# Low parts of the exponentials on GpSimd, and the values' low part as a full weight tile

## The chip, the cores and the metric

The kernel runs on one core of one Trainium2 chip. The metric is the device time of one execution in microseconds: 2285.27 us, the median of three runs (2280.55 to 2286.03). The profile of before is of a separate execution.

## The reference, cut to what matters

The model is a two-layer diffusion backbone over 1024 latent tokens and 256 context tokens, width 1024. Layer 0 runs grouped-query attention (8 query heads of 64, 2 key/value heads) beside a bidirectional mLSTM (4 heads of 128), then a mixture of 16 experts; layer 1 is a pooling mixer and a second mixture of experts. The change touches attention alone:

```python
qb = q.reshape(Bn, nb, Q_BLOCK, A_KV_HEADS, G, d).transpose(1, 0, 3, 4, 2, 5)   # G = 4 heads per key head
def one_block(qblk):
    s = jnp.einsum('bhgtd,bhsd->bhgts', qblk, kt).astype(jnp.float32) * scale
    p = jax.nn.softmax(s, axis=-1).astype(vt.dtype)
    return jnp.einsum('bhgts,bhsd->bhgtd', p, vt)
```

The keys and values are those of the 256 context tokens followed by the 1024 latent tokens, so each of the 8 heads weighs 1280 keys for 1024 queries. Everything is float32.

## The kernel before, in words

A float32 product is made of three faster matmuls. `split` (L57) writes a rounded high part (type fp32r) on ScalarE and the rest, source minus high part, on VectorE (L59, L60). A product is then high x high + high x low + low x high, each a matmul of fp32r operands. A plain float32 matmul is also used in places; it shows as two instructions.

The kernel runs in stages: projections of layer 0 (to about 390 us), `mixers` (attention and mLSTM, to about 732 us), `out0` (the output projection, norm and router), the experts of layer 0, `layer1`, and the experts of layer 1.

`attention_start` (L593) runs interleaved with the last projection. For each of the two key heads g it makes KS (keys, high part in partitions 0 to 63 and low part in 64 to 127), K2 (high part, and a row of ones for the bias), VA (128 keys x 10 tiles x 128: the values' high part in columns 0 to 63, ones in columns 64 to 127) and VL (128 x 10 x 64: the values' low part). They lie in the pool `kv`, allocated from the right end of SBUF.

`mixers` (L676) walks over the 8 heads. For head h, `weighted(h)` takes two query blocks of 512 and for each of them ten key tiles of 128. A tile is two matmuls for the scores (L703, L704) into one of two PSUM buffers `se`, the exponential on ScalarE (L706, `e`), and the weighted values into `po`, where rows 0 to 63 collect the output and rows 64 to 127 the sum of the weights. Three of the ten tiles (`WHOLE`: 2, 5, 8) use one plain float32 matmul of `e` with VF (L709). For the other seven, `e` is split into `eh` and `el`: by `split` (ScalarE and VectorE) in heads 0 to 6, and on VectorE alone (L717, L718) in head 7. Then come three matmuls: VA x eh (L719), VL x eh into rows 0 to 63 only (L720), and VA x el (L721). `e`, `eh` and `el` have three buffers each. Two block ends per head take a reciprocal of the sum through Ln and Exp (L724, L725), one product on VectorE (`oo`, L727) and a store.

Beside head h run the preparation of head h+1 (`queries`, L626; `largest`, L645: the scores once more, with a maximum per query on VectorE from PSUM, L659 and L664, and the maxima sent through a small DMA to the bias row of QB, L674, issued on GpSimd) and the steps of the mLSTM (`mlstm`, L764). On GpSimd there stand in this stage only the memsets of QB (L635), v (L774) and VF (L693) and that DMA.

The order of each engine's instructions is made before the run by the framework's scheduler: it takes the program's order as priority, issues what it finds ready by its own costs, and adds every wait. Each engine then executes its list in order. A tile's memory can be reused once the earlier tile there is released.

Of the kernel before, what the change touches and what calls it, by code (L numbers as in the profile page):

```python
# [11 lines left out]
F32 = mybir.dt.float32  # L12
F32R = mybir.dt.float32r
# [4 lines left out]
ALU = mybir.AluOpType  # L18
# [8 lines left out]
NTA = 10  # L27
# [16 lines left out]
class Kern:  # L44
# [548 lines left out]
    def attention_start(self, es, psp):  # L593

        tc, nc = self.tc, self.nc
        P = lambda name, bufs=1: es.enter_context(tc.tile_pool(name=name, bufs=bufs, side="right", reuse_waits="tile"))
        P("pad").tile([128, PADS[2]], F32, name="pad")
        kv, self.q0, self.qs = P("kv"), P("q0"), P("qs", 2)
        self.q1 = None
        self.at = self.sc = (psp, "tr")  # L600
        KS = self.KS = [kv.tile([128, 1280], F32R, name=f"KS{g}") for g in range(2)]
        K2 = self.K2 = [kv.tile([128, 1280], F32R, name=f"K2{g}") for g in range(2)]
        VA = self.VA = [kv.tile([128, NTA, 128], F32R, name=f"VA{g}") for g in range(2)]
        VL = self.VL = [kv.tile([128, NTA, 64], F32R, name=f"VL{g}") for g in range(2)]
        self.Q = {}
        for g in range(2):
            nc.gpsimd.memset(K2[g][64:128].bitcast(F32), 0.0)
            nc.gpsimd.memset(K2[g][64:65].bitcast(F32), 1.0)
            nc.gpsimd.memset(VA[g][:, :, 64:128].bitcast(F32), 1.0)
        for g in range(2):  # L610
            if g:
                self.queries(0)
                yield
                yield from self.largest(0)
            for c0, c1 in ((0, 4), (4, 8), (8, 10)):
                ps = self.at[0].tile([128, 512], F32, name=self.at[1], tag=self.at[1])
                for t in range(c0, c1):
                    nc.tensor.transpose(ps[0:64, (t - c0) * 128:(t - c0 + 1) * 128],
                                        self.KR[:, t, g * 64:(g + 1) * 64], self.idf)
                s = slice(c0 * 128, c1 * 128)  # L620
                self.halves(ps[0:64, :(c1 - c0) * 128], KS[g][0:64, s], K2[g][0:64, s], KS[g][64:128, s])
                yield
            self.split(VA[g][:, :, 0:64], VL[g], self.VR[:, :, g * 64:(g + 1) * 64])
            yield

    def queries(self, h):  # L626
# [48 lines left out]

    def mixers(self):  # L676
        tc, nc, I = self.tc, self.nc, self.I
        KS, K2, VA, VL, Q = self.KS, self.K2, self.VA, self.VL, self.Q
        with ExitStack() as es:
            P = lambda name, bufs=1, **k: es.enter_context(tc.tile_pool(name=name, bufs=bufs, reuse_waits="tile", **k))  # L680
            ml = P("ml", 2)
            pp, sp, self.q1 = P("p", 3), P("ast", 2), P("q1")
            ps_t, ps_s = P("ps_t", 1, space=PSUM), P("ps_s", 2, space=PSUM)
            ps_e, ps_o, ps_m = P("ps_e", 2, space=PSUM), P("ps_o", 1, space=PSUM), P("ps_m", 2, space=PSUM)
            self.at, self.sc = (ps_t, "at"), (ps_s, "sc")

            def weighted(h):

                QA, QB = Q.pop(h)
                g = h // 4  # L690
                if h % 4 == 0:
                    self.VF = sp.tile([128, len(WHOLE), 128], F32, name="VF", tag="VF", bufs=1)
                    nc.gpsimd.memset(self.VF[:, :, 64:128], 1.0)  # L693
                    for i, t in enumerate(WHOLE):
                        nc.vector.tensor_copy(self.VF[:, i, 0:64], self.VR[:, t, g * 64:(g + 1) * 64])
                VF = self.VF
                for q in range(2):
                    qs = slice(q * 512, (q + 1) * 512)
                    po = ps_o.tile([128, 512], F32, name="po", tag="po")
                    for t in range(NTA):  # L700
                        ts = slice(t * 128, (t + 1) * 128)
                        ps = ps_e.tile([128, 512], F32, name="se", tag="se")
                        nc.tensor.matmul(ps, KS[g][:, ts], QA[:, qs], start=True, stop=False)  # L703
                        nc.tensor.matmul(ps, K2[g][:, ts], QB[:, qs], start=False, stop=True)  # L704
                        e = pp.tile([128, 512], F32, name="e", tag="e")
                        nc.scalar.activation(e, ps, AF.Exp)  # L706
                        a, l = t == 0, t == NTA - 1
                        if t in WHOLE:
                            nc.tensor.matmul(po, VF[:, WHOLE.index(t)], e, start=a, stop=l, skip_group_check=True)  # L709
                            yield  # L710
                            continue
                        eh = pp.tile([128, 512], F32R, name="eh", tag="eh")
                        el = pp.tile([128, 512], F32R, name="el", tag="el")
                        if h < 7:
                            self.split(eh, el, e)
                        else:
                            nc.vector.tensor_copy(eh, e)  # L717
                            nc.vector.tensor_tensor(el, e, eh.bitcast(F32), op=ALU.subtract)  # L718
                        nc.tensor.matmul(po, VA[g][:, t], eh, start=a, stop=False, skip_group_check=True)  # L719
                        nc.tensor.matmul(po[0:64], VL[g][:, t], eh, start=False, stop=False, skip_group_check=True)  # L720
                        nc.tensor.matmul(po, VA[g][:, t], el, start=False, stop=l, skip_group_check=True)  # L721
                        yield
                    rc = sp.tile([64, 512], F32, name="rc", tag="rc")
                    nc.scalar.activation(rc, po[64:128], AF.Ln)  # L724
                    nc.scalar.activation(rc, rc, AF.Exp, scale=-1.0)  # L725
                    o = sp.tile([64, 512], F32, name="oo", tag="oo")
                    nc.vector.tensor_tensor(o, po[0:64], rc, op=ALU.mult)  # L727
                    nc.sync.dma_start(self.OT[h * 64:(h + 1) * 64, qs], o)

            M = self.mlstm_steps(ml, ps_m)  # L730
            for h in range(8):
                nxt = iter(())
                if h < 7:
                    self.queries(h + 1)
                    nxt = self.largest(h + 1)
                for i, _ in enumerate(weighted(h)):
                    for _ in range(2 if i % 5 == 0 else 1):
                        next(nxt, None)
                    if i % 5 == 4:
                        next(M, None)  # L740
            for _ in M:
                pass
# [910 lines left out]
```

## Time and profile before

| | |
|---|---|
| median of the runs | 2285.27 us (2280.55 to 2286.03) |
| the profiled execution | 2288.23 us |
| its span, first to last instruction | 2286.4 us |
| mean granted TensorE clock | 0.966 of 2.4 GHz |
| busy over the span | PE 93%, DVE 82%, ACT 62%, POOL 10% |

PE is TensorE, PEld its weight loads, DVE VectorE, ACT ScalarE, POOL GpSimd. A matmul's duration in the records includes its way through the array, so durations of successive matmuls overlap; how fast they follow each other is read from their starts. In the rows below, a wait is named by who waited, for what, and what released it; brackets in the timeline give the idle time of the engine before the instruction and what ended it.

### The profile page before, as it was taken

How to read it: one execution, taken by the hardware profiler on the slowest of the kernel's cores; microseconds unless marked ns; L12 is line 12 of the kernel's file. 1: busy time of each engine (PE TensorE's matmuls, PEld its weight loads, DVE VectorE, ACT ScalarE, POOL GpSimd, SP SyncE). 2: the span in 40 equal slices, each digit the busy share in tenths (PEclk: the TensorE clock that was granted, in tenths of full speed). 3: DMA queues.
4: the chain of work that ended last, by engine and by line, in shares of the span. 5: the costliest groups of instructions: out<-in, count | busy, mean ns of one | idle time of the engine just before them, and what ended most of it. 6: DMA issues, size and time to landing. Idle time of an engine off the chain costs nothing.

```text
span 2286.4 us, 29558 instructions
## 1 busy us (share of the span) xinstructions
PE 2120.9 (93%) x10371; PEld 1678.5 (73%) x10371; DVE 1884.3 (82%) x2936; ACT 1408.8 (62%) x2042; POOL 220.8 (10%) x345
## 2 busy tenths in 40 slices
PE   6889999999997988999999999899659999999997
PEld 3768887776664767788888877667548888888874
DVE  7888754888886557899999989844589999999986
ACT  6412314667774325788888877744337888888874
POOL 0111111000000011000000000012200000000001
PEclk9999999999998999999999999989869999999998
DMA  7576662243413658999999999513869999999964
GB/s 276 187 253 229 243 217 92 79 120 95 111 58 95 246 193 318 392 393 393 402 393 392 401 375 356 184 33 102 314 225 359 393 399 391 397 391 390 397 227 157
DMA packets 211738, 609.76 MB, mean 267 GB/s; under 512 B 17620, under 2 KB 62116, under 8 KB 210436
## 3 DMA queue, kind: packets, MB, share of 16 engines
q1 hardware_dynamic: 168800, 484.95, 56.0%
q0 software_dynamic: 22560, 79.61, 11.8%
q10 hardware_dynamic: 20228, 43.30, 5.2%
q8 instruction: 82, 1.34, 0.2%
q14 instruction: 68, 0.56, 0.1%
HBM read 550.11 MB, written 56.77 MB: 265 GB/s over the span
## 4 chain that ended last, share of the span: by engine, by line
PE 77%; DMA 8%; DVE 6%; issue 5%; ACT 3%; POOL 1%; ACTq 0%; POOLq 0%; DVEq 0%; SPq 0%
PE g L54 5%; PE g L55 5%; PE u L54 5%; PE g L53 5%; PE u L53 5%; PE d L54 5%; PE u L55 5%; PE d L55 5%; PE d L53 5%; DMA wm<-in_w_mod 2%; PE tr L1250 2%; PE pp L55 2%; PE pp L54 2%; PE pp L53 2%; PE po L709 2%
## 5 line engine op out<-in xcount | busy, mean ns | idle before, releaser
L60 DVE TENSOR_TENSOR wl<-R,wh 128x1024 fp32r<-128x1024 f32 x496 | 584.7, 1222 | 26.0 <-ACT wh L59 13.7
L59 ACT CAST wh<-R 128x1024 fp32r<-128x1024 f32 x496 | 518.1, 1055 | 131.1 <-PE g L55 43.0
L60 DVE TENSOR_TENSOR wl<-X,wh 128x1024 fp32r<-128x1024 f32 x182 | 215.9, 1222 | 13.8 <-ACT wh L59 8.7
L59 ACT CAST wh<-X 128x1024 fp32r<-128x1024 f32 x182 | 190.4, 1054 | 49.3 <-PE d L55 22.6
L53 PE MATMUL u<-wh,xh 128*128 128x512 f32 x512 | 202.7, 396 | 2.5 <-ACT wh L59 2.5
L53 PE MATMUL d<-wh,ah 128*128 128x512 f32 x512 | 201.8, 394 | 2.9 <-DVE o L1285 2.9
L53 PE MATMUL g<-wh,xh 128*128 128x512 f32 x512 | 202.6, 396 | 1.7 <-ACT xh L59 1.7
L54 PE MATMUL u<-wl,xh 128*128 128x512 f32 x512 | 201.2, 393 | 2.3 <-DVE wl L60 2.2
L54 PE MATMUL d<-wl,ah 128*128 128x512 f32 x512 | 200.5, 392 | 2.3 <-DVE wl L60 2.3
L54 PE MATMUL g<-wl,xh 128*128 128x512 f32 x512 | 200.8, 392 | 2.0 <-DVE wl L60 1.9
L55 PE MATMUL u<-wh,xl 128*128 128x512 f32 x512 | 200.6, 392 | 0.0
L55 PE MATMUL g<-wh,xl 128*128 128x512 f32 x512 | 200.3, 391 | 0.0
L55 PE MATMUL d<-wh,al 128*128 128x512 f32 x512 | 199.9, 390 | 0.0
L59 ACT CAST wh<-raw 128x1024 fp32r<-128x1024 f32 (+1 forms) x116 | 119.7, 1039 | 54.6 <-PE pp L55 12.4
L60 DVE TENSOR_TENSOR wl<-raw,wh 128x1024 fp32r<-128x1024 f32 (+1 forms) x116 | 135.9, 1204 | 11.6 <-ACT wh L59 8.8
L706 ACT ACTIVATE e<-se 128x512 f32<-128x512 f32 x160 | 91.5, 595 | 56.8 <-PE se L704 50.6
L54 PEld LDWEIGHTS u<-wl,xh 128*128 128x128 f32 x512 | 96.6, 189 | 24.0 <-DVE wl L60 4.8
L54 PEld LDWEIGHTS d<-wl,ah 128*128 128x128 f32 x512 | 96.3, 188 | 23.4 <-DVE wl L60 4.6
L53 PEld LDWEIGHTS d<-wh,ah 128*128 128x128 f32 x512 | 96.3, 188 | 22.8 <-ACT ah L59 3.7
L54 PEld LDWEIGHTS g<-wl,xh 128*128 128x128 f32 x512 | 96.5, 189 | 22.3 <-DVE wl L60 3.4
L53 PEld LDWEIGHTS u<-wh,xh 128*128 128x128 f32 x512 | 96.6, 189 | 22.2 <-ACT wh L59 2.9
L53 PEld LDWEIGHTS g<-wh,xh 128*128 128x128 f32 x512 | 96.5, 189 | 21.6 <-ACT xh L59 2.7
(523 smaller groups left out, 4710.8 us busy)
## 6 DMA issues: line engine op xcount, KB each, us to landing
R<-in_w_exp_gate SPq DMA_DIRECT2D x84, 1024.0 KB
R<-in_w_exp_down SPq DMA_DIRECT2D x82, 1024.0 KB
R<-in_w_exp_up SPq DMA_DIRECT2D x81, 1024.0 KB
wm<-in_w_mod POOLq DMA_DIRECT2D x80, 512.0 KB, 5.4
X<-in_w_exp_up SPq DMA_DIRECT2D x31, 1024.0 KB
X<-in_w_exp_gate SPq DMA_DIRECT2D x30, 1024.0 KB
X<-in_w_exp_down SPq DMA_DIRECT2D x30, 1024.0 KB
raw<-in_w_exp_up SPq DMA_DIRECT2D x16, 1024.0 KB
```

The source lines that it names most:

```text
L53: mm(ps, lh, rh, start=start, stop=False)
L54: mm(ps, lh, rl, start=False, stop=False)
L55: self.mark = mm(ps, ll, rh, start=False, stop=stop).ins
L59: self.nc.scalar.copy(hi, src)
L60: return self.nc.vector.tensor_tensor(lo, src, hi.bitcast(F32), op=ALU.subtract).ins
L706: nc.scalar.activation(e, ps, AF.Exp)
L709: nc.tensor.matmul(po, VF[:, WHOLE.index(t)], e, start=a, stop=l, skip_group_check=True)
L1250: nc.tensor.transpose(ps[:, j * 128:(j + 1) * 128], src[:, (4 * q + j) * 128:(4 * q + j + 1) * 128], self.idf)
```

## The change

In heads 0 to 6 the high part `eh` stays on ScalarE, and the subtraction that makes `el` is issued on GpSimd. Head 7 stays as it was. VL becomes a tile of 128 columns like VA; columns 64 to 127 are zero, and its matmul writes all 128 rows of `po`. VL moves from the pool `kv` (right side, allocated before the projections end) to the pool `ast` of `mixers` (left side), from 2 x 2560 to 2 x 5120 bytes a partition. Two memsets on GpSimd write the zeros; the subtraction that makes VL, formerly part of `split` in `attention_start`, is done on VectorE at the first head of each group. The copy of the high part into VA stays on ScalarE where it was.

```diff
@@ attention_start
-        VL = self.VL = [kv.tile([128, NTA, 64], F32R, name=f"VL{g}") for g in range(2)]
...
-            self.split(VA[g][:, :, 0:64], VL[g], self.VR[:, :, g * 64:(g + 1) * 64])
+            nc.scalar.copy(VA[g][:, :, 0:64], self.VR[:, :, g * 64:(g + 1) * 64])
@@ mixers
+            VL = [sp.tile([128, NTA, 128], F32R, name=f"VL{g}", bufs=1) for g in range(2)]
+            for g in range(2):
+                nc.gpsimd.memset(VL[g][:, :, 64:128].bitcast(F32), 0.0)
@@ weighted, where h % 4 == 0
+                    nc.vector.tensor_tensor(VL[g][:, :, 0:64], self.VR[:, :, g * 64:(g + 1) * 64],
+                                            VA[g][:, :, 0:64].bitcast(F32), op=ALU.subtract)
@@ weighted, per tile
                         if h < 7:
-                            self.split(eh, el, e)
+                            nc.scalar.copy(eh, e)
+                            nc.gpsimd.tensor_tensor(el, e, eh.bitcast(F32), op=ALU.subtract)
...
-                        nc.tensor.matmul(po[0:64], VL[g][:, t], eh, start=False, stop=False, skip_group_check=True)
+                        nc.tensor.matmul(po, VL[g][:, t], eh, start=False, stop=False, skip_group_check=True)
```

## Rows read from the trace of the kernel before

**Rows 1.** Windows, 400 to 700: length, busy us (count) by engine, clock, DMA.

```profile
400.00:700.00 300.00, 284.11 (x1400) 205.31 (x1399) 265.38 (x594) 214.06 (x498) 11.52 (x33) 0.99 0.34 92
```

**Rows 2.** Waits, 400 to 700: us in total, times, longest.

```profile
POOL v L774 <- PE mp L833: 174.2, 16, 17.0
...
POOL QB L674 <- DMA md<-mr: 46.4, 2, 38.1
...
PEld se L703 <- ACT e L706: 14.2, 29, 1.5
...
PEld po L721 <- DVE el L60: 4.1, 9, 1.5
...
PE po L721 <- DVE el L60: 1.5, 2, 1.0
PE se L704 <- DMA QB<-md: 1.5, 1, 1.5
...
PEld po L719 <- ACT e L706: 0.7, 3, 0.2
...
PE sc L663 <- DVE mx L659: 0.4, 1, 0.4
```

**Rows 3.** Groups by line and form, 400 to 700: busy us, mean ns, idle before.

```profile
L60 DVE TENSOR_TENSOR el<-e,eh 128x512 fp32r<-128x512 f32 x96 | 65.3, 685 | 4.4 <-ACT eh L59 4.1
...
L719 PEld LDWEIGHTS po<-eh,VA 128*128 128x128 f32 x96 | 18.1, 189 | 13.7 <-ACT eh L59 6.2 <-issue 2.2 <-DVE oo L727 2.1
...
L720 PEld LDWEIGHTS po<-eh,VL 128*64 128x64 f32 x96 | 13.1, 136 | 5.6 <-issue 4.3
...
L828 DVE TENSOR_TENSOR v<-v,g_col 128x516 f32<-128x516 f32 x17 | 11.8, 693 | 0.7 <-PE mp L814 0.5
...
L817 DVE TENSOR_TENSOR dn<-dn,g_col 128x2 f32<-128x2 f32 x32 | 4.9, 154 | 5.8 <-ACT dn L816 5.5
```

**Rows 4.** Groups by line and form, POOL, whole span.

```profile
L951 POOL TENSOR_TENSOR h<-h,r_a 128x1024 f32<-128x1024 f32 x2 | 4.7, 2334 | 0.1
...
L609 POOL MEMSET VA<- 128x640 f32 x2 | 1.3, 640 | 20.6 <-PE tr L574 17.4 <-DVE KS L748 3.1
...
L1047 POOL TENSOR_TENSOR res<-aff,tk 128x128 f32<-128x128 f32 x2 | 0.9, 459 | 0.0
```

**Rows 5.** Timeline, two split tiles near 505: start us, us, instruction.

```profile
503.84 0.61 ACT L59 CAST eh<-e 128x512 fp32r<-128x512 f32 x1
...
504.71 0.69 DVE L60 TENSOR_TENSOR el<-e,eh 128x512 fp32r<-128x512 f32 x1
...
505.45 0.19 PEld L721 LDWEIGHTS po<-el,VA 128*128 128x128 f32 x1
...
506.43 0.62 ACT L59 CAST eh<-e 128x512 fp32r<-128x512 f32 x1
...
507.99 0.69 DVE L60 TENSOR_TENSOR el<-e,eh 128x512 fp32r<-128x512 f32 x1
...
508.86 0.19 PEld L721 LDWEIGHTS po<-el,VA 128*128 128x128 f32 x1
```

**Rows 6.** Timeline, GpSimd and VectorE side by side near 856.

```profile
855.39 2.33 POOL L951 TENSOR_TENSOR h<-h,r_a 128x1024 f32<-128x1024 f32 x1
...
856.08 1.66 DVE L1019 TENSOR_TENSOR thr<-nxt,tm 128x4 int32<-128x4 int32 x1
857.67 0.15 DVE L997 TENSOR_TENSOR base<-base,tm 128x1 int32<-128x1 int32 x1
```

**Rows 7.** Timeline, PE, matmuls of one tile in a row, near 722.

```profile
722.11 0.39 PE L719 MATMUL po<-eh,VA 128*128 128x512 f32 x1
722.34 0.39 PE L720 MATMUL po<-eh,VL 128*64 128x512 f32 x1
722.56 0.39 PE L721 MATMUL po<-el,VA 128*128 128x512 f32 x1
```

**Rows 8.** Timeline, VectorE after the end of attention.

```profile
736.99 0.29 DVE L892 TENSOR_TENSOR wp<-wr,a2c 128x128 f32<-128x128 f32 x1 [4.72 <-DMA wr<-in_w_router]
```

More of the change, by code (lines that the diff above doesn't have):

```diff
@@ L677, in mixers @@
         tc, nc, I = self.tc, self.nc, self.I
-        KS, K2, VA, VL, Q = self.KS, self.K2, self.VA, self.VL, self.Q
+        KS, K2, VA, Q = self.KS, self.K2, self.VA, self.Q
         with ExitStack() as es:
```

## The prediction

> **What bounds the kernel now.** I read the page's busy shares first, then the stages by windows, then the waits, the groups and the timeline of the stage that the diff touches. The reader is to see in the busy shares only that no engine is the limit of the whole span; the change lies in one stage. From 400 to 700 us the heads before the last run beside the mLSTM steps. There DVE works 265.4 of 300 us (88%), ACT 214.1, PE is marked busy for 284.1, and GpSimd for 11.5 [rows 1]. So this stage has a nearly full DVE and an empty GpSimd, and the change takes work from the first to the second.
>
> A full engine need not be the one that the path waits for, so the waits decide. PE executes its instructions in a fixed order, and a wait of PE or of its weight load is lost time unless the matmul before it is still streaming. In this stage eight such groups of waits are ended by ACT, from 14.2 for the score buffers that the exponential still reads down to 0.7: 37.5 us. Eleven groups are ended by DVE: from 4.1 for `el` down to 0.4 for a maximum, together 16.0, of which `el` itself is 4.1 + 1.5 = 5.6 in 11 cases [rows 2]. PE thus waits for ACT more than twice as much as for DVE, although DVE is the fuller one. That is what keeps my forecast small: at most 16.0 us can go directly, and 53.5 if ACT's waits went too.
>
> **The change part by part.**
>
> *The subtraction leaves DVE.* In heads 0 to 6 fourteen query blocks have seven split tiles each, 98 in all; 96 of them start in the window, at 685 ns: 65.3 us [rows 3]. DVE falls to 200.1 us of 300.
>
> *It arrives on GpSimd.* The trace has no subtraction of 128x512 there. It has the two-source form at 128x128 (459 ns) and at 128x1024 (2334 ns) [rows 4]; these are the bounds. A straight line between them gives 459 + 384/896 x 1875 = 1263 ns, which I take, since both ends are the same kind of operation and the new one lies between; that the output is now fp32r is not in any row. 98 x 1.263 = 124 us, on an engine with 288 us free here: throughput is no limit. Latency is: each low part takes 1.263 - 0.685 = 0.58 us longer.
>
> *Who feels these 0.58 us.* Two tiles show both answers [rows 5]. The first `eh` ends at 504.45, DVE begins 0.26 later, and PE loads `el` at 505.45, at once when it is there; GpSimd would finish at about 505.76, 0.3 us late. The second `eh` ends at 507.05, DVE is in other work until 507.99 and delivers at 508.68; GpSimd would deliver at about 508.4, earlier than DVE, and PE asks for it only at 508.86. Bounds: none of the low parts is late, or all 96 are by the whole difference, 56 us. Only 11 of 96 wait today, so I am near the lower end: these 11 cost 6.4 us more; a fresh queue without DVE's backlog gives about a third of it back, +4 us.
>
> *A lock beside it.* While GpSimd's multiplication at 855.39 reads its two SBUF sources, DVE's 128x4 tensor operation takes 1.66 us and ends as GpSimd ends; a like one behind it takes 0.15 [rows 6]. So a DVE operation with two SBUF sources stands still until GpSimd is through. In the window eight groups have two such sources (v, E twice, wi, the output projection's low parts, hs, ob, dn): 141 instructions, 73.5 us; the first and the last are in [rows 3]. GpSimd will be in a subtraction 96 x 1.263 / 300 = 40% of the time, with 0.63 us left on average: 141 x 0.40 x 0.63 = 36 us more on DVE. Bounds 0 and 96 x 1.263 = 121 us, if every subtraction held DVE throughout. I take the 36: DVE 236 of 300, 79% instead of 88%. So more than half of what DVE seems to gain is taken back.
>
> The Trainium skill, "SBUF — State Buffer", section "Who interferes with whom", says that it goes the other way too: whichever comes first holds the pair, so a subtraction can also stand behind DVE. No row shows GpSimd held; by that rule each would meet such an operation with chance 73.5/300, about 0.1 us on average or 9 us of latency over all, most of it in tiles that PE doesn't yet ask for.
>
> *GpSimd's queue.* It runs in order, too, and today its waits cost nothing because nothing stands behind them: 174.2 us in 16 waits of the v memset for PE, and 46.4 in 2 of the query bias load for a small DMA [rows 2]. Now subtractions stand behind them, and behind each subtraction that waits for `eh` the next QB and v memsets and the bias load, for which the next head's scores wait. The order is made ahead of the run from when things become ready, so a subtraction should not stand long behind a later event: 0 at best, 23 such instructions (16 and 7) with 1.26 us each at worst, 29; I take 0, since PE waits for the bias load once, 1.5 us.
>
> *The freed DVE.* DVE's other results (maxima, wi, oo) come earlier. Of 10.4 us that PE waits for them I let two thirds go, -7: the load of DVE that is left is 79%. ACT, too, waits for DVE (E, sq, the e buffers held by `el`), and the exponentials behind these are what PE waits for longest; of the 37.5 us I let a fifth go, -7. Bounds: 0 and -10.4 for the first, 0 and -37.5 for the second.
>
> *VL over the whole array.* The weight load grows from 136 to 189 ns (the full one of VA) [rows 3], which stays under the matmul beside it: they start 0.23 us apart in [rows 7]. Matmuls of 512 columns take the same time at 64 and at 128 columns of weights, so nothing is added. It removes the change between a half and a full array, 224 times. In [rows 7] full, half and full follow each other at 0.23 and 0.22 us, so there is nothing to remove: 0. If that cover is gone (a stalled matmul that waits for its own weights), it costs 0.05 us a time, 6 us at most. The Trainium skill, "TensorEngine Tiling (Array Packing)", section "Key Properties", says that changing the mode drains the array; by it the edit alone would win much, and I carry that as a rival.
>
> *The edits with one answer.* The copy into VA stays on ACT; the two VL subtractions go from the projections to the first head of each group, and two memsets on GpSimd of VA's size (0.64 each, [rows 4]) come before head 0. 0 to 2 us; I take 0, since GpSimd and DVE have nothing else to do for a head that has no `eh` yet. VL's new place (5 KB a partition more on the left and less on the right) shifts where the output projection's first tiles lie. After attention DVE stands 4.72 us for the router weights, with the low parts that PE needs next queued behind [rows 8]: such a wait may move by about 3 us either way; I take 0.
>
> **The sum.** -7 - 7 + 4 = -10 us. The profiled execution took 2288.2 (span 2286.4 and 1.8 around it), 3 above the median of 2285.3. So 2278 in its terms, 2275 as a median. Later stages begin earlier by the same.
>
> **The rivals.**
>
> 1. *The low parts come too late (slower).* Place: the PE matmul of `el`. If half of the 96 are late by the whole 0.58 us, that is 28 us, less the 14 gained: +14, 2299; with DVE's lock on top of each (0.25) +26, 2311. It decides from about 24 late tiles on (14/0.58). For it: GpSimd is nearly twice as slow, three buffers of e, eh and el are held longer, and pairs of `eh` 0.62 us apart queue behind one 1.26 us subtraction. Against it: 85 of 96 don't wait today, and PE has other matmuls ready.
>
> 2. *Nothing comes of it.* PE waits for ACT, ACT keeps its 214 us, and DVE simply idles more: gain and delay cancel within 7 us, 2285. For it: 37.5 against 16.0 us in the waits. Against it: DVE at 88% also sets when E, wi and the maxima come.
>
> 3. *The change of array mode does cost.* If each switch made PE wait for the 0.39 us that a matmul lasts instead of 0.23, 224 switches cost 36 us, and the time would be 2275 - 36 = 2239. Against it stand the starts in [rows 7].
>
> **How the numbers follow.** Forecast 0.45, rival 1 0.30, rival 2 0.22, rival 3 0.03. About 0.3%, 7 us, is what can be told from no change. The forecast and rival 3 are faster: 0.48; same 0.22; slower 0.30. The forecast's own range is 2256 to 2278: twice the gain with more of ACT's waits, or hardly any. The full range reaches over rival 2 to rival 1 without most of its lock: 2253 to 2303. Beyond it lie rival 3, a gain that needs ACT's waits to go almost entirely, and the dearer half of rival 1.
>
> **What would show it.** Right: DVE's busy time from 400 to the end of the stage falls by less than 65 us, because tensor operations with two SBUF sources show means above 0.69 us; GpSimd's subtractions at 1.2 to 1.4 us; PE's waits for maxima, wi and oo shrink; the VL matmuls keep 0.39 us and their spacing 0.23; the last head ends about 10 us earlier. Wrong: PE's waits for `el`, now ended by GpSimd, above 20 us; GpSimd waiting long for PE or the small DMA with subtractions behind it; subtractions near 2 us; or the VL edit alone moving the time.

## The result: slower by 54 us, and the profile after

The changed kernel takes 2338.74 us (median of four runs, 2334.64 to 2343.12) against 2284.64 of the kernel before on the same chip (four runs, 2280.55 to 2286.03): ratio 1.0241, interval 1.0226 to 1.0257. The prediction was 2275, with 2303 as the upper end: wrong in its sign and outside its range.

The loss has one place. The first load that reads the last head's output (its first 256 queries; `OT` holds the attention's output) starts at 721.2 us before and at 769.2 us after: 48 us later. The lines of the two kernels:

```profile
L1078 SPq DMA_DIRECT2D R<-OT x1: 372/372/372, 721.2 to 721.2; - x1
```

```profile
L1083 SPq DMA_DIRECT2D R<-OT x1: 373/373/373, 769.2 to 769.2; - x1
```

The rest of the kernel is 2 us shorter in the profiled executions. Their spans, 2286.4 and 2332.7, differ by 46 us and not by the 54 of the medians, since the profiled execution after was the fastest of its four.

The window from 400 to 700 us of the kernel after, with the columns of [rows 1]:

```profile
400.00:700.00 300.00, 263.16 (x1261) 184.38 (x1260) 214.03 (x460) 181.01 (x440) 120.13 (x112) 0.99 0.29 82
```

VectorE is relieved, as meant: 214 us where it was 265. But TensorE starts 1261 matmuls in the window where it started 1400, and ScalarE works 181 us where it worked 214. The granted clock is 0.99 in both. Every engine but GpSimd idles more, so this is not a matter of throughput but of a chain of waits. The waits of the same window, as in [rows 2], here the longest of them and the lines that answer to those of before:

```profile
POOL el L720 <- ACT eh L719: 115.3, 46, 8.0
ACT e L710 <- PE se L708: 62.2, 42, 4.0
PEld po L726 <- POOL el L720: 47.0, 56, 1.5
POOL v L779 <- PE mp L838: 36.6, 13, 6.0
PE po L726 <- POOL el L720: 26.6, 46, 1.0
...
PEld mp L865 <- DVE hs L862: 5.5, 5, 1.6
...
PEld se L707 <- ACT e L710: 4.9, 15, 0.5
...
PEld po L726 <- POOL v L779: 2.8, 4, 1.1
```

The two lines for `po` and `el` are the change: PE's weight load waits for the low part 56 times, 47.0 us, where it waited 9 times, 4.1 us; PE itself, once its weights are there, waits 46 times, 26.6 us, where it waited twice, 1.5 us [rows 2]. The wait for the score buffers went the other way, from 14.2 to 4.9 us: TensorE now comes to them late enough. The page's chain of work that ended last names the same place; GpSimd's subtraction has 2% of the span in it (2.5%, some 58 us, when the chain is asked for by itself). That is all its time on the chain and not what the change added:

```profile
PE u L53 5%; PE u L54 5%; PE d L54 5%; PE u L55 5%; PE g L54 5%; PE d L55 5%; PE g L55 5%; PE g L53 5%; PE d L53 5%; POOL el L720 2%; PE tr L1255 2%; DVE wl L60 1%; DMA R<-in_w_exp_gate 1%; PE z L53 1%; PE y L53 1%
```

Groups of the same window by line and form, for [rows 3]:

```profile
L720 POOL TENSOR_TENSOR el<-e,eh 128x512 fp32r<-128x512 f32 x81 | 110.4, 1369 | 141.9 <-ACT eh L719 115.3 <-ACT dn L821 12.8 <-ACT mr L670 6.0
...
L726 PE MATMUL po<-el,VA 128*128 128x512 f32 x81 | 38.9, 481 | 28.7 <-POOL el L720 26.6 <-POOL v L779 1.8
...
L725 PE MATMUL po<-eh,VL 128*128 128x512 f32 x81 | 32.6, 403 | 0.0
...
L725 PEld LDWEIGHTS po<-eh,VL 128*128 128x128 f32 x80 | 15.3, 191 | 3.3 <-issue 2.2
...
L833 DVE TENSOR_TENSOR v<-v,g_col 128x516 f32<-128x516 f32 x16 | 13.2, 823 | 1.3 <-DMA v<-VB 0.6 <-POOL el L720 0.3 <-issue 0.2
...
L822 DVE TENSOR_TENSOR dn<-dn,g_col 128x2 f32<-128x2 f32 x32 | 10.3, 322 | 3.2 <-ACT dn L821 3.1
```

81 subtractions start where 96 did. VectorE's operations with two SBUF sources are longer (`v` 693 to 823 ns, `dn` 154 to 322). And two tiles of the timeline, beside [rows 5]:

```profile
502.16 0.50 PE L724 MATMUL po<-eh,VA 128*128 128x512 f32 x1
502.16 0.68 DVE L811 TENSOR_TENSOR wi<-wi,qT 128x512 f32<-128x512 f32 x1
502.18 1.78 POOL L720 TENSOR_TENSOR el<-e,eh 128x512 fp32r<-128x512 f32 x1 [2.90 <-ACT eh L719]
...
504.02 0.50 PE L726 MATMUL po<-el,VA 128*128 128x512 f32 x1 [0.91 <-POOL el L720]
...
510.06 1.28 POOL L720 TENSOR_TENSOR el<-e,eh 128x512 fp32r<-128x512 f32 x1
510.29 0.40 PE L725 MATMUL po<-eh,VL 128*128 128x512 f32 x1
...
510.52 0.40 PE L708 MATMUL se<-QB,K 128*128 128x512 f32 x1
...
511.39 0.50 PE L726 MATMUL po<-el,VA 128*128 128x512 f32 x1 [0.48 <-POOL el L720]
```

In the second tile a subtraction of 1.28 us starts beside the first high matmul, the order puts one score matmul between, and PE then stands 0.48 us. In the first tile GpSimd meets VectorE's `wi`, which began 0.02 us earlier, takes 1.78 us in place of 1.28, and PE stands 0.91 us.

### The profile page after: what moved, and what is told of

The parts are those of the page before. It is cut to its first block, busy times and chain, and to the rows that moved or that the text cites. A ratio compares the mean times of both kernels' runs of the same rounds, so it can differ in the third digit from the quotient of the medians.

```text
span 2332.7 us, 29633 instructions
## 1 busy us (share of the span) xinstructions
PE 2138.4 (92%) x10371; PEld 1680.7 (72%) x10371; DVE 1862.3 (80%) x2838; ACT 1411.2 (60%) x2042; POOL 361.1 (15%) x445
## 4 chain that ended last, share of the span: by engine, by line
PE 59%; issue 5%; DVE 4%; DMA 3%; POOL 3%; ACT 2%; POOLq 0%; ACTq 0%; SPq 0%; DVEq 0%
PE u L53 5%; PE u L54 5%; PE d L54 5%; PE u L55 5%; PE g L54 5%; PE d L55 5%; PE g L55 5%; PE g L53 5%; PE d L53 5%; POOL el L720 2%; PE tr L1255 2%; DVE wl L60 1%; DMA R<-in_w_exp_gate 1%; PE z L53 1%; PE y L53 1%
## 5 line engine op out<-in xcount | busy, mean ns | idle before, releaser
L720 POOL TENSOR_TENSOR el<-e,eh 128x512 fp32r<-128x512 f32 x98 | 138.4, 1419 | 171.6 <-ACT eh L719 144.9
L1263 POOL DMA_INDIRECT xg<-G,ci x32 | 36.6, 1144 | 636.7 <-PE tr L1255 457.1
L1294 POOL DMA_INDIRECT X<-o,ci x30 | 48.4, 1612 | 471.1 <-DVE o L1290 471.1
```

Source lines behind the costliest of these rows:

```text
L720: nc.gpsimd.tensor_tensor(el, e, eh.bitcast(F32), op=ALU.subtract)
L1263: nc.gpsimd.indirect_dma_start(out=xg, out_offset=None, in_=self.G, in_offset=bass.IndirectOffsetOnAxis(ap=IX[e][0], axis=0))
L1294: nc.gpsimd.indirect_dma_start(out=self.X, out_offset=bass.IndirectOffsetOnAxis(ap=IX[e][0], axis=0), in_=o, in_offset=None, compute_op=AL ...
```

## The experiments

Medians and ratios are against the kernel before on the same chip. The kernel before had medians of 2280.9 to 2286.4 on these chips, so a difference of two runs from different chips is sure to a few us only. "Stage end" is the start of the first load that reads the last head's output, in the profiled execution (before 721.2, after 769.2).

**The two halves of the change alone.** First only VL's shape and place, with the subtraction left on VectorE; then only the subtraction on GpSimd.

```diff
-                        nc.tensor.matmul(po[0:64], VL[g][:, t], eh, ...)
+                        nc.tensor.matmul(po, VL[g][:, t], eh, ...)      # VL full, zeros in columns 64 to 127
```

> VL as a full zero-padded tile in its new pool, the subtraction back on VectorE. Theory A (the loss is that TensorE waits for low parts that come late from GpSimd): 2285, within 7 us of before. Theory B (the full-width VL or its new place costs, through its memory or the order): a good part of the 54 us stays, 2305 or more. Theory of the array mode (the half-width matmul costs a switch): 2250 or less.

```diff
-                            self.split(eh, el, e)
+                            nc.scalar.copy(eh, e)
+                            nc.gpsimd.tensor_tensor(el, e, eh.bitcast(F32), op=ALU.subtract)
```

> VL as before (64 columns, old pool), the low parts of heads 0 to 6 on GpSimd. Theory A: the whole loss, 2330 to 2345, with TensorE and its weight load waiting some 55 us for el in the attention stage. Theory B: near before, 2285 to 2295.

Measured: 2281.04, ratio 0.9996 (0.9979 to 1.0012), and 2339.11, ratio 1.0257 (1.0233 to 1.0281). VL over the whole array costs and gives nothing; the whole loss is GpSimd's subtraction.

**Is it that the low part comes late?** The low matmul is issued one key tile later, in the kernel after and in the kernel before.

```diff
...
-                        nc.tensor.matmul(po, VA[g][:, t], el, start=False, stop=l, skip_group_check=True)
+                        while held:                         # the low part of the tile before
+                            nc.tensor.matmul(po, *held.pop(), start=False, stop=False, skip_group_check=True)
+                        if l:
+                            nc.tensor.matmul(po, VA[g][:, t], el, start=False, stop=True, skip_group_check=True)
+                        else:
+                            held.append((VA[g][:, t], el))
```

> The changed kernel, but the matmul of each low part is issued one key tile later, after the next tile's high-part matmuls (in all heads), so TensorE has other work while GpSimd subtracts. Theory A: TensorE's waits for el fall from some 55 us to under 15, and most of the loss goes: 2275 to 2300. Theory C (the shared port: VectorE held by GpSimd and GpSimd by VectorE slows the whole stage): the lock is untouched, 2325 or more.

> The kernel before with the same hold of one tile, low parts on VectorE: the control for the hold itself. Theory A: TensorE waited only 5.6 us for el there, so 2278 to 2288. If the hold alone gains over 10 us, a gain of the run before it in this list is not the cure of late low parts alone.

Measured: 2309.13, ratio 1.0120 (1.0102 to 1.0138), and 2291.91, ratio 1.0047 (1.0029 to 1.0066). The hold gives 30 us back where GpSimd subtracts, and costs some 8 where VectorE does (5 at the stage's end, 726.2). Then GpSimd subtracts with VL as before, and the low matmul is issued two tiles later, with four buffers of `el`; and GpSimd subtracts in three tiles of seven, whose low matmul is issued behind the next key tile:

> Low parts on GpSimd with VL as before, the low matmul held for two key tiles, one more buffer of el. Theory A (what is left after the hold of one tile is still lateness: 21 us of waits for el): those waits under 8 us and 2285 to 2300. Theory C (what is left is the shared port and VectorE's longer operations): 2305 or more, as with one tile.

```diff
-                            nc.gpsimd.tensor_tensor(el, e, eh.bitcast(F32), op=ALU.subtract)
+                            (nc.gpsimd if t in (1, 4, 7) else nc.vector).tensor_tensor(el, e, ...)
...
```

> The kernel before, but in heads 0 to 6 the low parts of key tiles 1, 4 and 7 alone (42 of 98) are made on GpSimd, and their matmul is issued behind the plain float32 tile that follows. Theory A: these have time, so little is lost, and VectorE is relieved by 29 us: 2275 to 2290. Theory C: the port is held 54 us, nearly half of the loss of 25 us that the hold of one tile left: 2292 to 2300.

Measured: 2304.9, ratio 1.0081 (1.0064 to 1.0097), and 2301.18, ratio 1.0072 (1.0055 to 1.0089). More hold does not bring the rest back: 15 to 19 us stay. The second has only 42 subtractions on GpSimd and still pays 15; there PE's weight load also waits 8.0 us in 16 cases for the low parts that VectorE makes, and what more goes into it stays open.

**What is left: VectorE held at the port?** "The port" is short for the lock of the prediction: a GpSimd operation that reads SBUF and a VectorE operation with two SBUF sources hold each other up. First VectorE makes the low parts again and nobody waits for GpSimd, which subtracts beside it; then, in place of GpSimd's subtraction, two memsets of `el` stand ahead of VectorE's, which read nothing; then there is no subtraction at all.

```diff
                             self.split(eh, el, e)
+                            junk = pp.tile([128, 512], F32R, name="gj", tag="gj", bufs=1)
+                            nc.gpsimd.tensor_tensor(junk, eh.bitcast(F32), el.bitcast(F32), op=ALU.subtract)
```

> The kernel before, low parts on VectorE, and behind each of the 98 an extra GpSimd subtraction of the same size that nothing reads: it leaves the path to TensorE and keeps the shared port and the buffers. Theory A: 2285 to 2297, from VectorE's operations that meet it. Theory C: 2310 or more, most of the 54 us.

```diff
+                            for _ in range(2):
+                                nc.gpsimd.memset(el.bitcast(F32), 0.0)
                             self.split(eh, el, e)
```

> The kernel before with two GpSimd memsets of el ahead of each of the 98 subtractions of VectorE: GpSimd is about as long busy as in the run with unread subtractions, but reads nothing. If the 22 us there came from the shared port: 2282 to 2292 here. If they came from GpSimd's queue and the buffers held longer: 2300 or more.

```diff
-                            self.split(eh, el, e)
+                            nc.scalar.copy(eh, e)
+                            el = eh
```

> The kernel before with the subtraction left out in heads 0 to 6; the low matmul streams eh once more, so TensorE's work stays. VectorE loses 65 us of the stage, GpSimd does nothing, no port is shared. It measures what relieving VectorE is worth at best. By the prediction's terms (7 + 7, and the 5.6 of waits for el): 2265 to 2272. If VectorE's fullness is not what TensorE waits for: 2278 to 2288.

Measured: 2307.74, ratio 1.0095 (1.0071 to 1.0119); 2285.84, ratio 1.0005 (0.9989 to 1.0021); 2275.9, ratio 0.9957 (0.9941 to 0.9974). GpSimd work that reads SBUF costs 22 us though nobody waits for it; work that only writes costs nothing. Not all of the 22 is the port on other operations: VectorE's own low parts come later too (828 ns for 685), and PE waits for them, where it waited 1.5 us:

```profile
PE po L723 <- DVE el L60: 9.5, 14, 2.0
```

And with VectorE freed of all 98 subtractions, nothing in their place, no more than 10 us are won.

**Port and lateness, each by itself.** Both kernels have no subtraction on VectorE in heads 0 to 6. In the first GpSimd's result isn't read; in the second and third GpSimd clears the exponentials' tile in three memsets, and the low matmul streams that tile, or `eh` instead.

```diff
-                            self.split(eh, el, e)
+                            nc.scalar.copy(eh, e)
+                            nc.gpsimd.tensor_tensor(el, e, eh.bitcast(F32), op=ALU.subtract)
+                            el = eh
```

> The run without the subtraction (2276), plus GpSimd's subtraction behind each of the 98 high parts, which nothing reads; the low matmul streams eh. The shared port is used as in the changed kernel, and no low part is late. If the port is the main cost: 2300 or more. If it is the smaller part: 2283 to 2297. If it costs nothing here: 2273 to 2280.

```diff
...
-                            self.split(eh, el, e)
+                            nc.scalar.copy(eh, e.bitcast(F32))
+                            for n in (512, 512, 128):
+                                nc.gpsimd.memset(e[:, :n].bitcast(F32), 0.0)
+                            el = e
```

> The run without the subtraction, plus three GpSimd memsets (together 1.28 us, nothing read) over e once eh is copied from it; the low matmul streams that and so waits 1.28 us behind eh, as in the changed kernel, without the shared port. The low parts are zeros. If lateness with VectorE relieved is the larger part: 2300 to 2315, with TensorE's waits for e above 35 us. If lateness costs only together with the port: 2273 to 2285.

> As the run before it, but the low matmul streams eh and does not wait for the memsets: the control, GpSimd as long busy and e held as long. 2273 to 2282 by both theories; above 2290 the buffers of e or GpSimd's queue would be a third cause.

Measured: 2298.07, ratio 1.0057 (1.0036 to 1.0079); 2280.49, ratio 0.9986 (0.9974 to 0.9997); 2277.83, ratio 0.9973 (0.9962 to 0.9984). So the port is worth 2298.1 - 2277.8 = 20 us. VectorE from 390 to 800 us with GpSimd reading, by line and form:

```profile
L808 DVE TENSOR_TENSOR wi<-wi,qT 128x512 f32<-128x512 f32 x16 | 16.3, 1017 | 0.0
...
L830 DVE TENSOR_TENSOR v<-v,g_col 128x516 f32<-128x516 f32 x18 | 15.8, 876 | 3.2 <-DMA v<-VB 3.0
...
L859 DVE SCALAR_TENSOR_TENSOR hs<-hs,mnr,ob 128x128 f32<-128x128 f32 x32 | 12.7, 439 | 0.1
```

and with GpSimd only writing (the third kernel):

```profile
L831 DVE TENSOR_TENSOR v<-v,g_col 128x516 f32<-128x516 f32 x18 | 12.4, 690 | 3.5 <-DMA v<-VB 3.2 <-issue 0.3
...
L809 DVE TENSOR_TENSOR wi<-wi,qT 128x512 f32<-128x512 f32 x16 | 11.1, 693 | 0.2 <-DMA wi<-MW 0.2
...
L860 DVE SCALAR_TENSOR_TENSOR hs<-hs,mnr,ob 128x128 f32<-128x128 f32 x32 | 9.6, 345 | 0.1
```

PE's own waits show where much of the 20 goes. In the stage (330 to 820 us), with GpSimd reading:

```profile
PE mp L835 <- DVE dn L820: 4.7, 6, 1.6
...
PE po L721 <- ACT eh L715: 4.2, 9, 1.2
...
PE mp L862 <- DVE hs L859: 3.7, 4, 1.8
...
PE mp L835 <- DVE dn L819: 2.9, 3, 1.3
```

and with GpSimd only writing, where PE has no wait for `hs`:

```profile
PE po L722 <- ACT eh L715: 1.5, 2, 1.0
...
PE mp L836 <- DVE dn L821: 0.9, 4, 0.3
...
PE mp L836 <- DVE dn L820: 0.2, 1, 0.2
```

That is 13 us more for `dn`, `hs` and `eh`.

The surprise is the second kernel: low parts as late as GpSimd's subtraction makes them (two memsets of 0.53 us and one of 0.20) cost 3 us, not 30. One memset behind VectorE's subtraction had cost nothing either:

```diff
                             self.split(eh, el, e)
+                            nc.gpsimd.memset(el.bitcast(F32), 0.0)
```

> The kernel before with one GpSimd memset of el behind each of the 98 subtractions of VectorE (the low parts are zeroed), and the low matmul waits for it: about 0.6 us more until el is ready, as with GpSimd's subtraction, with nothing read by GpSimd and VectorE as full as before. Theory A (lateness is the larger half): 2305 to 2320, with waits of TensorE for el of 30 us or more. If the loss needs the shared port: 2282 to 2295.

Measured: 2281.67, ratio 0.9976 (0.996 to 0.9993).

**So when does lateness cost?** The kernels differ in TensorE's order, which is made ahead of the run from planned durations. With VectorE's subtraction 34 of the 112 split tiles have no matmul between the one with VL and the low one; with the three memsets 32; with GpSimd's subtraction 68. A first try to change that order traced the next tile's scores ahead of the low matmul:

```diff
...
+                        with tc.issue_after(behind):      # the next tile's score matmul
+                            nc.tensor.matmul(po, VA[g][:, t], el, ...)
```

> Low parts on GpSimd, VL as before; the score matmuls of the next key tile are put before the low matmul of this one in TensorE's order, in all heads. If the order is what turned 1.28 us into waits: 2298 to 2312, with waits of TensorE for el under 25 us. If the port makes low parts late whatever the order: 2325 or more.

> The same order with the low parts on VectorE, the control: 2280 to 2292, near before. Well below 2278 the order would be a gain of its own, and the run before it would have to be read against this one.

Measured: 2331.23, ratio 1.0220 (1.0195 to 1.0245), and 2279.42, ratio 0.9992 (0.9982 to 1.0002). The edit missed its aim: the scores went ahead of the high matmuls too, and 75 tiles have nothing between. It decides nothing.

The second try lengthens what is planned for GpSimd. Two columns of the low part are made twice again, or four times, which makes the order roomier (42 and 37 tiles with nothing between) and the result later. Beside it, GpSimd's subtraction is replaced by one memset; TensorE's order is then that of the kernel with GpSimd's subtraction but for some 40 of 6000 instructions compared.

```diff
...
                             nc.gpsimd.tensor_tensor(el, e, eh.bitcast(F32), op=ALU.subtract)
+                            for _ in range(2):
+                                nc.gpsimd.tensor_tensor(el[:, :2], e[:, :2], eh[:, :2].bitcast(F32), op=ALU.subtract)
```

> The values' low part stands as before; GpSimd makes every low part of heads 0 to 6 (98) and then makes two of its columns twice again, so the low matmul waits still longer than with GpSimd's subtraction alone; nothing is left out. What differs is TensorE's order: of 112 split tiles 42 have nothing between the matmul with the values' low part and the low matmul (34 before, 68 with the subtraction alone), and on the average there are 1.5 (0.7 with the subtraction alone, 2.7 before, by one count). Theory (the order sets what the lateness costs): relief -8, port +20, lateness with room +3 to +8, so 2300 to 2310, in spite of the later low parts. Rival (the lateness itself is what costs, whatever the order): later by some 0.3 us in each tile than with the subtraction alone at 2339, so 2345 or more.

> As the run with two columns made twice again, but four times: the low parts come later again, and 37 of 112 tiles have nothing between (2.1 on the average). Theory (order): no slower than that run by more than 5 us, 2298 to 2312. Rival (lateness): slower than that run by another 5 to 15 us, 2350 or more.

> No subtraction in heads 0 to 6: the low matmul streams a tile of zeros that one GpSimd memset of 128x512 (0.53 us) writes over the exponentials once their high part is copied. TensorE's order has the same counts as with GpSimd's subtraction alone: nothing between in 68 of 112 tiles, 0.7 on the average. No port in it, and 0.53 us of lateness in place of 1.28. Theory (the tight order is laid out for a low part that is some half a microsecond late, and what costs is the 0.75 us that it comes later than that): 2272 to 2284, no worse than the memsets that nobody waits for (2278) by over 6 us. Rival (the tight order costs by itself, or any lateness in it): 0.53 of 1.28 of the 35 us, 15 us over those memsets, 2290 to 2296.

Measured: 2373.2, ratio 1.0404 (1.0381 to 1.0426); 2403.32, ratio 1.0536 (1.0517 to 1.0556); 2280.2, ratio 0.9988 (0.9975 to 1.0002). My theory, that the count of tiles with room between sets the cost, falls: with room for more tiles both became slower than with GpSimd's subtraction alone, by 34 and by 64 us. But the rival, that lateness costs whatever the order, doesn't hold for the three memsets or the one. What does hold in all of them is in the waits of the stage (330 to 820 us) for the low part. The kernel after:

```profile
PEld po L726 <- POOL el L720: 57.3, 63, 2.6
...
PE po L726 <- POOL el L720: 34.1, 53, 2.2
```

The kernel with two columns made twice again, and the one with four times:

```profile
PEld po L724 <- POOL el L718: 92.1, 68, 3.1
...
PE po L724 <- POOL el L718: 67.7, 57, 2.6
```

```profile
PEld po L724 <- POOL el L718: 113.0, 70, 3.3
...
PE po L724 <- POOL el L718: 87.0, 65, 3.0
```

The hold of two tiles, the three memsets, and the one memset:

```profile
PEld po L705 <- POOL el L725: 18.3, 25, 1.5
...
PE po L705 <- POOL el L725: 9.2, 16, 1.2
```

```profile
PEld po L725 <- POOL e L718: 15.4, 47, 1.4
...
PE po L725 <- POOL e L718: 2.1, 5, 1.1
```

```profile
PEld po L725 <- POOL e L718: 8.1, 26, 0.4
```

The PE line (the matmul itself, not its weight load, of which part lies under the matmul before) goes with the stage's end. The stage ends at 714.4 us with neither cost, and at 736.6 with the port alone. The two kernels with memsets are to be compared with the first, the others with the second (the hold of one tile has three lines, 5.5 + 3.4 + 2.9):

| kernel | stage end | later than its base | PE's wait for the low part |
|---|---|---|---|
| three memsets | 714.4 | 0.0 | 2.1 |
| one memset | 714.9 | 0.5 | 0 |
| hold of two tiles | 746.0 | 9.4 | 9.2 |
| hold of one tile | 747.0 | 10.4 | 11.8 |
| scores between | 763.5 | 26.9 | 29.0 |
| after | 769.2 | 32.6 | 34.1 |
| GpSimd's subtraction, VL as before | 772.3 | 35.7 | 34.6 |
| two columns twice again | 807.5 | 70.9 | 67.7 |
| two columns four times again | 837.2 | 100.6 | 87.0 |

In the last row 14 us are left over; its 392 small subtractions read SBUF too. For the two holds the agreement is in part luck, since the hold by itself costs 5 us at the stage's end.

Why the roomier order didn't help stands in the timeline of the kernel with two columns made twice again:

```profile
500.07 1.28 POOL L716 TENSOR_TENSOR el<-e,eh 128x512 fp32r<-128x512 f32 x1 [0.75 <-ACT eh L715]
...
501.43 0.47 POOL L718 TENSOR_TENSOR el<-e,eh 128x2 fp32r<-128x2 f32 x2
...
502.24 0.48 PE L724 MATMUL po<-el,VA 128*128 128x512 f32 x1
...
506.79 2.50 POOL L716 TENSOR_TENSOR el<-e,eh 128x512 fp32r<-128x512 f32 x2 [1.56 <-ACT eh L715]
...
509.25 1.56 POOL L718 TENSOR_TENSOR el<-e,eh 128x2 fp32r<-128x2 f32 x4
...
510.71 0.51 PE L724 MATMUL po<-el,VA 128*128 128x512 f32 x1 [2.55 <-POOL el L718]
```

At 500 the order has enough between, and a low part that is whole 1.86 us after the first high matmul began costs nothing. At 506.8 GpSimd works off two tiles in a row, then four small subtractions, the first two of 0.66 and 0.64 us beside operations of VectorE and the others of 0.19: 4 us until the first tile's low part is whole, and PE stands 2.55 us. So what counts, by these tiles and the table, is by how much the result comes later than this tile's place in the order allows, not how many tiles have some room.

## Why the prediction was wrong

The sum was -7 - 7 + 4. Measured, with neither port nor lateness -6 (2277.8), the port +20 (2298.1), the lateness of GpSimd's subtraction some +41 (2338.7, on another chip); at the stage's end -7, +22 and +33.

*Who feels these 0.58 us* is the step that failed: +4 was taken, and it is 33 to 41. The step counted who waits in the trace of before, 11 of 96 [rows 2], and carried that order over. But TensorE's order is remade when an instruction changes its engine. In the new one twice as many tiles have the low matmul right behind VL's, as if GpSimd delivered in half a microsecond: one memset of 0.53 us in the subtraction's place leaves nearly the same order, and there it costs nothing. The subtraction takes 1.28. That it is planned for so short is inferred from this likeness, not shown. Rival 1 names this mechanism, with half of the tiles late by 0.58 us; it was about as many (53 of 98 by PE's line), but the comparison is not with VectorE's duration: each stood 0.64 us on average. So rival 1 had the size of this term; what it lacked is the next one.

*A lock beside it* has the right mechanism and nearly the right size, and its price was put to the wrong account. The 36 us of VectorE time are 23 between the two kernels without and with the port (the differences of the means by the counts: `wi` 5.2, `v` 3.3 and `hs` 3.0 from the rows shown, and E 5.6, `dn` 3.9, `ob` 2.2). Two operations of the mLSTM's norm with two SBUF sources (L79, L81, 128x4) were missing from the list; they add 2.7 and 4.8, so 31 in all. The 36 were set against VectorE's relief, as if an engine at 79% had time for them. Yet the path paid 20 to 22. So the maxima and copies that VectorE no longer delays are worth little, and the mLSTM's operations that it now holds are on the way: PE's waits for `dn`, `hs` and `eh` above make up 13 of the 20. Which waits make up the rest isn't settled. That GpSimd is held in turn was carried in the sentence on the Trainium skill ("SBUF — State Buffer", "Who interferes with whom"): the trace agrees, with 1.78 and at most 3.07 us for a subtraction of 1.28, and 1419 ns on average, 13 us over all, close to the 9 worked out there. The same section of the Trainium skill says that a VectorE instruction with two SBUF inputs doesn't contend with a GpSimd instruction that only writes SBUF; the two memsets agree, at ratio 1.0005 and with 684 ns for `wi`.

*The freed DVE*: -14 was taken, -6 to -10 came (neither cost, and no subtraction at all). The reading that PE waits for ACT more than for VectorE was right, and should have been carried further: rival 2 was the better base.

*Right*: GpSimd's duration (1263 ns from the line between two sizes; median 1284, though the output is fp32r); the queue of GpSimd (PE's weight load waits 2.8 us for the `v` memset behind it); VL at 0 (403 ns a matmul, 191 ns a load under it), which refutes rival 3 with the ratio 0.9996; and the wait for the router weights after attention, 2.43 us where it was 4.72 [rows 8], inside the 3 us allowed.

The marks set for "wrong" were met: PE's waits for the low part above 20 us. The chance of 0.30 for slower had the right cause, but its price (2299 to 2311) left the lock on the path out except as 0.25 us a tile. How much of the 33 to 41 us comes from the order and how much from GpSimd being held is not settled by a run, since no kernel had the port, this lateness and the roomier order of the three memsets at once. The trace of the kernel after, read tile by tile, bounds it. In the 59 tiles where PE stood until a low part had come, 36 us together, the time beyond 1.28 us of a subtraction makes up at most 9 us, and with it a late start on GpSimd at most 16. The other 20 us fall on subtractions that began at once and took their usual time: there the order expects the low part too early.

## What to carry to other kernels

Moving an operation to a slower engine changes the order of the engine that waits for it: price the whole duration from source to consumer against the new order, not the difference against the old one. Before moving two-source work from VectorE to GpSimd, list the VectorE operations with two SBUF sources that will run beside it and put most of their lengthening on the path; here 20 of 31 us were on it, two to three times what the freed 65 us of VectorE gave. Test the price with an unread copy of the operation on the new engine and the old one left out: it shows the port's part without the wait's. Where the old one stays, its own result is held too, and the wait is in the price.

## What the runs showed of the hardware

- 98 subtractions of 128x512 on GpSimd, whose result nobody reads, cost 20 and 22 us (two pairs of kernels; the 22 with VectorE's own low parts held, too); 196 memsets of the same size cost 0 (ratio 1.0005), though they take 1.05 us of GpSimd a tile beside 1.28.
- The holding goes both ways: GpSimd's subtraction 1261 ns at least and 3067 at most, VectorE's `wi` took 686 ns on average before and 957 to 1076 beside it.
- A two-source GpSimd subtraction of only 128x2 takes 0.19 us at least and up to 1.22 us: the small ones are held as well. With four a tile, the 197 that began beside no VectorE operation took 0.195 us (median), the 102 beside a maximum (one source, in PSUM) as much, and those beside `wi`, E, v and `ob` 0.52 to 0.58, ending 0.05 us after that operation.
- Matmuls of fp32r with 64 and with 128 columns of weights follow each other alike, 0.23 us apart; making them all full changed nothing that can be measured.
